# A hybrid decoder layer: z's projection in products of 512 columns, its Silu functions split around q's first copies, and two step quotas altered

## The chip, the core and the metric

The kernel runs on one core of a Trainium2 chip. A core has a matrix engine (TensorE, PE in the profile; its weight loads are shown apart as PEld), a vector engine (VectorE, DVE), an engine for functions and copies (ScalarE, ACT), a general one (GpSimd, POOL) and one that issues transfers (SyncE, SP). Each engine issues its instructions in a fixed order of its own, and engines wait for each other through semaphores. Products go to PSUM, a small memory that TensorE writes and DVE and ACT read; everything else lies in SBUF. The metric is the device time of one execution in microseconds; the kernel before is judged by the median of 3 runs.

## What is computed

One layer over 256 positions of 1024 channels, all in float32: a half-weighted SwiGLU network, then a Mamba-2 branch (SSD) and a differential attention branch side by side, gated and merged, then a second SwiGLU network, each with a norm before and behind it. The part that the change touches:

```python
u = rmsnorm(h, mix_pre_g[l])
z, xbc, dt_raw, q, k, v, gate_logits = jnp.split(u @ w_in[l], IN_SPLITS, axis=-1)
...
y = ssd_chunked(xh, dt, a_head, bm, cm)
y = (y + d_skip[:, None] * xh).astype(z.dtype)
y = y.reshape(b, L, SSD_D_INNER) * jax.nn.silu(z)
y = rmsnorm(y.reshape(b, L, SSD_GROUPS, SSD_D_INNER // SSD_GROUPS), 1.0).reshape(b, L, SSD_D_INNER) * norm_g
return y @ w_branch
```

z has 2048 columns, q and k 1024 each, the gates 2048. The SSD works in 4 groups of 8 heads, the attention in 8 heads.

## The kernel before

Every float32 weight and activation is split into a high part (rounded to the fast type float32r) and a low part (the rest), and a product is the sum hi x hi + hi x lo + lo x hi. Weights come from HBM in chunks of 1 MB through three `raw` buffers; for each half of a chunk ACT writes `whi` (a cast, line 250) and DVE writes `wlo` (a subtraction, line 253). `take()` hands out a chunk and prepares those that follow, three ahead. A raw buffer is loaded anew, on SP's queue, once its chunk is split.

There are two ways to make a 256-column chunk of the transposed projections. `mm_t` (line 294) writes both halves m of a chunk into one PSUM bank and takes 24 products of 256 columns for each half: 8 of `wh` with the high part of u, 8 with the low part, then 8 of `wl` with the high part. `mm_w` (line 306) lays the high and low parts of u side by side: for each half m, in a bank of its own, 8 products of `wh` with 512 columns and 8 of `wl` with 256 columns. Its bank then holds two sums, so ACT copies the right one to SBUF and DVE adds the left one. Three banks (`pj`) serve all of these. B, C, x and z are made by `mm_t`; q, k and the networks' gate and up by `mm_w`.

The mixer goes through its chunks in this order: v, B and C, x (8 chunks, tile `xs`), z (8 chunks, `pz` to `sz`), q and k in turn (4 chunks each, `pq` and `pk`), the gates (8 chunks, `pgt`), the SSD branch's output (8 chunks, `pws`), the attention branch's output (4 chunks, `pwd`), and the merge's output (`acc_mx`).

Behind these, in small steps, runs the background work. `Background.run(us)` (line 1298) adds `us` to an account and takes steps off a queue until the account is used up; each step names its own price. The queue holds first `cb_work`, then `ssd_work` for groups 0 to 3, then `ssd_norm`, then `att_work`. A group of `ssd_work` is: X (8 transposes `px` on TensorE, two DVE products), four E steps (each with eight 128-column functions and clips on ACT and DVE, an Exp of 512 columns on ACT and a product with `cbm` on DVE; every other one first loads `acb`, 512 KB, through POOL's queue), and `py` (32 products that read the E of all four steps, the last one first, then four DVE operations into `xs`). A group of `ssd_norm` multiplies `xs` by Silu of z, squares, sums into `ssum`, forms `pn` with two products by a matrix of ones, takes Ln and Exp, scales `xs` and splits it into `yh` and `yl`, which `pws` needs. `att_work` makes the heads' scores `psc`, the softmax, the transposes `pa`, the values `po` and the turned pairs `pto`.

What a chunk leaves to the background is set by four constants: `BG_US` 3.15 for each chunk of z, `QK_US` 2.4 for each of q and k, `GATE_US` 1.75 for each of 16 calls in the gates, `SSD_US` 1.55 for each of 16 calls in the SSD branch and 4 in the attention branch's first half.

ACT keeps one set of function tables at a time. `act_table(name)` loads another set and keeps the functions before and behind it apart; Silu is in one set, Exp and Ln in another, Sigmoid in a third. z's four Silu (one for each group, lines 1334 and 1335) stand between two such loads.

From x to k a scheduler chooses each engine's order by its own estimates of when things are ready. From the gates on, TensorE's order is the program's (`own_order(PE)`, line 1351); the other engines' orders are still the scheduler's.

Of the kernel before, what the change touches and what calls it, by code (L numbers as in the profile page):

```python
# [18 lines left out]
AF = mybir.ActivationFunctionType  # L19
# [4 lines left out]
EXP_LN = "natural_log_exp_and_others"  # L24
# [3 lines left out]
T = 256  # L28
# [12 lines left out]
WARM = 3  # L41
FILL = 2
TAIL = 3
BG_US = 3.15
QK_US = 2.4
GATE_US = 1.75
SSD_US = 1.55
DOWN = {"f1": "p q1 p p q2 p ppp", "f2": "q1 p q2 p q3 ppp"}
FIRST, LAST = (1, 2, 3, 5, 7, 6, 4), (1, 6, 7, 2, 5, 3, 4)
BREAK, STOP = object(), object()  # L50
# [3 lines left out]
def tile_hybrid_layer(ctx: ExitStack, tc: tile.TileContext, x, ffn1_pre_g, ffn1_w_gate, ffn1_w_up,  # L54
# [4 lines left out]
    nc = tc.nc  # L59
# [5 lines left out]
    def k4(shape, name, dt=F32):  # L65
        return sb.tile(shape, dt, tag="k4", name=name, bufs=K4_BUFS)
# [4 lines left out]
    def k2(shape, name, dt=F32):  # L71
        return sb.tile(shape, dt, tag="k2", name=name, bufs=K2_BUFS)
# [7 lines left out]
    def pj(name):  # L80

        return ps.tile([P, 512], F32, tag="pj", name=name, bufs=3)

    def pjt(name):

        return pj(name).rearrange("p (m t) -> p m t", m=2)

    def bg(shape, name):
        return ps.tile(shape, F32, tag="bg", name=name, bufs=5)
# [169 lines left out]
    def split_to(n):  # L259

        while len(splits) < min(n, len(units)):
            of, p = units[len(splits)]
            if p is not None:
                splits.append(of.split(p))
                continue
            for _ in split_steps():
                pass

    def ahead_of(i, n):

        n *= 4
        while n > 0 and i < len(units):
            n -= 4 if units[i][1] is None else 1
            i += 1
        return i

    def take(ahead=AHEAD):

        i = taken[0]
        taken[0] += 1  # L280
        split_to(ahead_of(i, ahead))
        (of, p), w = units[i], splits[i]
        splits[i] = None
        if p is not None:
            return w
        his, los = w
        nj = chunks[of][1][1] // 2
        return (lambda j: his[j // nj][:, j % nj, :], lambda j: los[j // nj][:, j % nj, :])
# [5 lines left out]
    def mm_t(acc, w, act, k0=0, first=True, last=True, ks=range(KD)):  # L294

        (wh, wl), (ah, al, _) = w, act
        acc = acc if isinstance(acc, list) else [acc[:, m, :] for m in range(2)]
        for m in range(2):
            cs = slice(m * P, (m + 1) * P)
            for j in ks:  # L300
                nc.tensor.matmul(acc[m], wh(j)[:, cs], ah(k0 + j), start=first and j == ks[0], stop=False)  # L301
                nc.tensor.matmul(acc[m], wh(j)[:, cs], al(k0 + j), start=False, stop=False)  # L302
            for j in ks:
                nc.tensor.matmul(acc[m], wl(j)[:, cs], ah(k0 + j), start=False, stop=last and j == ks[-1])  # L304

    def mm_w(dst, name, w, act, scale=None):


        (wh, wl), (ah, _, ahl) = w, act
        for m in range(2):  # L310
            acc = pj(f"{name}{m}")
            cs = slice(m * P, (m + 1) * P)
            for j in range(KD):
                if j:
                    nc.tensor.matmul(acc[:, :T], wl(j)[:, cs], ah(j), start=False, stop=False)  # L315
                nc.tensor.matmul(acc, wh(j)[:, cs], ahl(j), start=j == 0, stop=j == KD - 1)  # L316
                if not j:
                    nc.tensor.matmul(acc[:, :T], wl(j)[:, cs], ah(j), start=False, stop=False)
            if scale is None:
                nc.scalar.copy(dst[:, m, :], acc[:, T:])  # L320
                nc.vector.tensor_tensor(dst[:, m, :], acc[:, :T], dst[:, m, :], ALU.add)  # L321
            else:
                nc.scalar.activation(dst[:, m, :], acc[:, T:], AF.Copy, scale=scale)
                nc.vector.scalar_tensor_tensor(dst[:, m, :], acc[:, :T], scale, dst[:, m, :], ALU.mult, ALU.add)

    def mm_nat(acc, w, act, k0, first, last, late):
# [25 lines left out]
    order = mybir.DependencyInfo(mybir.DependencyClass.NoSync, mybir.DependencyReason.DATA)  # L352

    def act_table(name):
        f = nc.scalar.preload_act_table_set(name)
        for prev in act_since:
            tc.add_manual_dep(f.ins, prev, order, reason="activation table")
        act_since.clear()
        act_fence[0] = f.ins.name

    def act(*args, **kw):
        a = nc.scalar.activation(*args, **kw)
        if act_fence[0] is not None:
            tc.add_manual_dep(a.ins, act_fence[0], order, reason="activation table")
        act_since.append(a.ins.name)
# [65 lines left out]
    def new_u(tag):  # L431
        for i in range(2):
            uT[i] = sb.tile([P, 4, 2, T], F32R, tag="u8", name=f"u{i}_{tag}", bufs=2)

    act_u = (lambda j: uT[j // 4][:, j % 4, 0, :], lambda j: uT[j // 4][:, j % 4, 1, :],
             lambda j: uT[j // 4][:, j % 4, :, :])
# [594 lines left out]
    for i in range(4):  # L1031
        acc = pjt(f"pbc{i}")
        mm_t(acc, take(), act_u)
        dst = (bT, cT)[i // 2]
# [16 lines left out]
    sz = [None] * 4  # L1051
# [52 lines left out]
    def ssd_norm(groups):  # L1104

        def one(g):
            nc.vector.tensor_tensor(xs[g], xs[g], sz[g], ALU.mult)
            sq = k4([P, 4, T], f"sqy{g}")
            nc.scalar.activation(sq, xs[g], AF.Square)
            yield 1.2  # L1110
            nc.vector.tensor_tensor(sq[:, 0:2, :], sq[:, 0:2, :], sq[:, 2:4, :], ALU.add)
            nc.vector.tensor_tensor(sq[:, 0, :], sq[:, 0, :], sq[:, 1, :], ALU.add)
            ssum = k2([P, 2, T], f"ssum{g}", F32R)
            split(ssum[:, 0, :], ssum[:, 1, :], sq[:, 0, :])
            yield 1.5
            yield BREAK
            pn = bg([P, T], f"pn{g}")
            for i in range(2):
                nc.tensor.matmul(pn, ones_r, ssum[:, i, :], start=i == 0, stop=i == 1)
            rs = sq[:, 1, :]  # L1120
            act(rs, pn, AF.Ln, scale=1.0 / 512, bias=eps_c)
            act(rs, rs, AF.Exp, scale=-0.5)
            yield 0.1
            for c in range(4):
                n = col["ng"] + g * 4 + c
                nc.vector.scalar_tensor_tensor(xs[g][:, c, :], xs[g][:, c, :], cols_a[:, n:n + 1], rs,
                                               ALU.mult, ALU.mult)
            yh[g] = k4([P, 4, T], f"yh{g}", F32R)
            yl[g] = k4([P, 4, T], f"yl{g}", F32R)
            split(yh[g], yl[g], xs[g])  # L1130
            xs[g] = sz[g] = None
            yield 2.8

        todo = [one(g) for g in groups]
        under_way = []
        while todo or under_way:
            if todo and len(under_way) < 2:
                under_way.append(todo.pop(0))
            for w in list(under_way):
                us = next(w, None)  # L1140
                if us is None:
                    under_way.remove(w)
                else:
                    yield us
# [170 lines left out]
    back = Background()  # L1315
    back.add(cb_work())
    for g in range(4):
        xs[g] = k4([P, 4, T], f"xs{g}")
        for i in range(2):
            acc = pjt(f"pxs{g}{i}")  # L1320
# [5 lines left out]
    for g in range(4):  # L1326
        sz[g] = k4([P, 4, T], f"sz{g}")
        for i in range(2):
            acc = pjt(f"pz{g}{i}")
            mm_t(acc, take(), act_u)  # L1330
            nc.scalar.copy(sz[g][:, i * 2:i * 2 + 2, :], acc)
            back.run(BG_US)
    act_table(SILU)
    for g in range(4):
        act(sz[g], sz[g], AF.Silu)
    act_table(EXP_LN)
    back.add(ssd_norm(range(4)))
    for c in range(4):
        if c % 2 == 0:
            qT[c // 2] = k4([P, 4, T], f"q{c}")  # L1340
            kT[c // 2] = k4([P, 4, T], f"k{c}")
        o = (c % 2) * 2
        mm_w(qT[c // 2][:, o:o + 2, :], f"pq{c}", take(), act_u, 0.125)
        back.run(QK_US)
        mm_w(kT[c // 2][:, o:o + 2, :], f"pk{c}", take(), act_u)
        back.run(QK_US)
# [42 lines left out]
    for q in range(2):  # L1389
# [3 lines left out]

        natural(f"pws{q}", 4, lambda j: yh[j // 4][:, j % 4, :], lambda j: yl[j // 4][:, j % 4, :], gated, SSD_US)
    yh = yl = None
# [18 lines left out]
    for q in range(2):  # L1414
# [4 lines left out]
        def merge(b, acc):  # L1419
# [5 lines left out]
        natural(f"pwd{q}", 2, lambda j: oh[j // 4][:, j % 4, :], lambda j: ol[j // 4][:, j % 4, :], merge,  # L1425
                SSD_US if q == 0 else 0.0, (attended, lambda: turn_merged(2))[q])

    pg = load_gain(mix_post_g, "pg_mx")
    acc = [[bg([P, 512], f"acc_mx{b}{q}") for q in range(2)] for b in range(2)]
# [47 lines left out]
```

## Time and profile before

| | us |
|---|---|
| median of 3 runs | 737.97 (737.88 to 738.38) |
| the profiled execution | 737.54 |
| its span, first to last instruction | 735.8 |
| first z product to first q product | 289.28 to 343.87 |
| q and k, to the first gates product | 343.87 to 395.86 |
| gates, to the first product of the SSD branch | 395.86 to 447.68 |
| SSD branch, to the first product of the attention branch | 447.68 to 501.08 |

The page divides the span among engines, into forty slices, and along the chain of work that ended last. A tile's name in a row (`pz`, `sz`, `E`) says which step an instruction belongs to, and `<-` in brackets says what ended the idle time before it. Since TensorE's instructions overlap, the pace of its products is read from start to start and not from the duration of one.

### The profile page before, as it was taken

The page shows a single profiled execution, that of the slowest core. Times are in us where ns is not written, and L with a number is a line of the kernel's source. Part 1 is how long each engine was busy: PE and PEld are TensorE (multiplying, and loading weights), DVE is VectorE, ACT ScalarE, POOL GpSimd, SP SyncE. Part 2 cuts the span into 40 slices and gives each one's busy share as a digit, 9 for nine tenths or more (in the row PEclk, how much of TensorE's full clock was granted, in tenths as well). Part 3 has the DMA queues.
Part 4 walks back from the last instruction along what each step waited for, and adds up shares of the span by engine and source line. Part 5 has one row for each costly group of instructions (what it writes and reads, how often), then busy time and mean ns, then how long its engine had stood idle before and what let it go on. Part 6 is the DMA issues. An engine that isn't in the chain of part 4 may idle for free.

```text
span 735.8 us, 10869 instructions
## 1 busy us (share of the span) xinstructions
PE 726.4 (99%) x4211; PEld 628.1 (85%) x4211; DVE 591.9 (80%) x904; ACT 462.1 (63%) x777; POOL 38.6 (5%) x72
## 2 busy tenths in 40 slices
PE   8999999999999999999999999999999999999996
PEld 6888888888889999999888788888888888888874
DVE  7978768998677878787996998785784878779994
ACT  7657556665566565958975577782663657566562
POOL 2700000000300000000000000000010000000000
PEclk9999999999999999999999999999999999999998
DMA  8884674469353647567464664475470765664541
GB/s 299 229 261 150 218 229 171 155 216 348 118 172 117 201 143 226 192 188 226 146 219 154 202 222 138 152 238 191 127 241 34 229 199 153 222 217 143 188 168 57
DMA packets 94212, 137.96 MB, mean 187 GB/s; under 512 B 2684, under 2 KB 68304, under 8 KB 94160
## 3 DMA queue, kind: packets, MB, share of 16 engines
q1 hardware_dynamic: 91488, 129.51, 54.2%
q0 software_dynamic: 2368, 7.22, 3.1%
q8 instruction: 33, 0.54, 0.3%
q10 hardware_dynamic: 304, 0.53, 0.2%
q14 instruction: 19, 0.16, 0.1%
HBM read 136.17 MB, written 1.08 MB: 187 GB/s over the span
## 4 chain that ended last, share of the span: by engine, by line
PE 97%; DVE 2%; issue 1%; DMA 0%; ACT 0%; DVEq 0%
PE pup_f L316 9%; PE pg_f L316 9%; PE pgt L335 6%; PE pws L335 6%; PE acc_f1p L625 5%; PE acc_f2p L625 4%; PE pg_f L315 4%; PE pup_f L315 4%; PE pn_f L335 3%; PE pn_mx L335 3%; PE acc_mx L573 3%; PE pn_f L345 3%; PE pwd L335 3%; PE acc_f1p L573 3%; PE pz L302 2%; PE pxs L304 2%
## 5 line engine op out<-in xcount | busy, mean ns | idle before, releaser
L253 DVE TENSOR_TENSOR wlo<-raw,whi 128x1024 fp32r<-128x1024 f32 (+1 forms) x226 | 266.6, 1208 | 22.7 <-ACT whi L250 21.7
L250 ACT CAST whi<-raw 128x1024 fp32r<-128x1024 f32 (+1 forms) x225 | 226.2, 1044 | 18.1 <-DMA raw<-in_w_in_dram 3.8
L316 PE MATMUL pup_f<-u_f,whi 128*128 128x512 f32 x288 | 101.3, 396 | 0.0
L316 PE MATMUL pg_f<-u_f,whi 128*128 128x512 f32 x288 | 101.2, 396 | 0.0
L315 PE MATMUL pg_f<-u_f,wlo 128*128 128x256 f32 x252 | 70.6, 280 | 0.0
L315 PE MATMUL pup_f<-u_f,wlo 128*128 128x256 f32 x252 | 70.3, 279 | 0.0
L316 PEld LDWEIGHTS pup_f<-u_f,whi 128*128 128x128 f32 x288 | 52.8, 188 | 9.8
L316 PEld LDWEIGHTS pg_f<-u_f,whi 128*128 128x128 f32 x288 | 52.8, 188 | 9.6
L315 PEld LDWEIGHTS pg_f<-u_f,wlo 128*128 128x128 f32 x252 | 47.5, 188 | 1.7
L315 PEld LDWEIGHTS pup_f<-u_f,wlo 128*128 128x128 f32 x252 | 47.5, 189 | 1.6
L321 DVE TENSOR_TENSOR su_f<-pup_f,su_f 128x256 f32<-128x256 f32 x36 | 15.1, 420 | 26.0 <-ACT su_f L320 25.8
L130 ACT CAST wqh<-wt 128x1024 fp32r<-128x1024 f32 x20 | 21.0, 1052 | 23.2 <-DVE wt L122 23.2
L320 ACT COPY su_f<-pup_f 128x256 f32<-128x256 f32 x36 | 13.4, 373 | 35.1 <-PE pup_f L316 34.9
L335 PE MATMUL pgt<-whi,u_mx 128*128 128x512 f32 x128 | 33.1, 393 | 0.0
L301 PE MATMUL pxs<-u_mx,whi 128*128 128x256 f32 x128 | 31.7, 285 | 0.0
L302 PE MATMUL pz<-u_mx,whi 128*128 128x256 f32 x128 | 31.6, 284 | 0.0
L301 PE MATMUL pz<-u_mx,whi 128*128 128x256 f32 x128 | 31.6, 284 | 0.0
L302 PE MATMUL pxs<-u_mx,whi 128*128 128x256 f32 x128 | 31.4, 283 | 0.0
L335 PEld LDWEIGHTS pgt<-whi,u_mx 128*128 128x128 f32 x128 | 23.6, 188 | 5.4 <-issue 0.7
L1009 DVE SCALAR_TENSOR_TENSOR xs<-pxs,cols_b,xs 128x255 f32<-128x255 f32 (+2 forms) x48 | 21.9, 475 | 6.3 <-ACT xs L1006 5.9
L291 ACT CAST gh_f<-sg_f 128x512 fp32r<-128x512 f32 x18 | 11.2, 622 | 21.5 <-DVE sg_f L771 21.5
L302 PEld LDWEIGHTS pz<-u_mx,whi 128*128 128x128 f32 x128 | 24.5, 192 | 0.2 <-issue 0.2
(397 smaller groups left out, 1698.5 us busy)
## 6 DMA issues: line engine op xcount, KB each, us to landing
raw<-in_w_in_dram SPq DMA_DIRECT2D x40, 1024.0 KB, 5.4
raw<-in_ffn_w_down_dram SPq DMA_DIRECT2D x22, 1024.0 KB, 4.9
raw<-in_ffn_w_gate_dram SPq DMA_DIRECT2D x20, 1024.0 KB, 5.6
raw<-in_ffn_w_up_dram SPq DMA_DIRECT2D x20, 1024.0 KB, 5.4
raw<-in_ssd_w_branch_dram SPq DMA_DIRECT2D x8, 1024.0 KB, 5.3
acb<-acd POOLq DMA_DIRECT2D x8, 512.0 KB, 5.5
raw<-in_da_w_branch_dram SPq DMA_DIRECT2D x4, 1024.0 KB, 5.1
raw<-in_w_out_dram SPq DMA_DIRECT2D x4, 1024.0 KB, 5.0
```

The costliest lines, as they stand in the source:

```text
L130: nc.scalar.copy(hi, src)
L250: copy(hi[:, js, :], r[:, q * nj + j:q * nj + j + n, :])
L253: nc.vector.tensor_sub(lo[:, js, :], r[:, q * nj + j:q * nj + j + n, :], hi[:, js, :].bitcast(F32))
L301: nc.tensor.matmul(acc[m], wh(j)[:, cs], ah(k0 + j), start=first and j == ks[0], stop=False)
L302: nc.tensor.matmul(acc[m], wh(j)[:, cs], al(k0 + j), start=False, stop=False)
L315: nc.tensor.matmul(acc[:, :T], wl(j)[:, cs], ah(j), start=False, stop=False)
L316: nc.tensor.matmul(acc, wh(j)[:, cs], ahl(j), start=j == 0, stop=j == KD - 1)
L335: nc.tensor.matmul(acc, a(k0 + j), b(j), start=first and i == 0, stop=last and i == 11)
L345: nc.tensor.matmul(accs[b], x_(k0 + j), w_(j), start=first and j == 0 and w_ is wh and x_ is acts[b][0], stop=last and j == 3 and w_ is wl)
L573: nc.tensor.matmul(acc[b][q], x_[:, ts], w_(kt)[:, halves[q]], start=begin and i == 0 and kt == 0 and x_ is ah and w_ is wh, stop=i == n - ...
L625: nc.tensor.matmul(bank[p], x_, w_, start=p not in begun, stop=last and p in (1, 5, 6, 7))
L1009: nc.vector.scalar_tensor_tensor(dst[:, m, s:], acc[:, m, :T - s], cw(3 - s, c), dst[:, m, s:], ALU.mult, ALU.add)
```

## The change

z's chunks are made by `mm_w`, so each half has a bank of its own, an ACT copy and a DVE addition. Silu of z's first group stays behind z; the other three are put behind q's first chunk and, on ACT, behind the last copy of that chunk (`last_copy`), and the load of the Exp set and the start of `ssd_norm` follow them. `BG_US` goes from 3.15 to 2.5 and `SSD_US` from 1.55 to 1.95.

```diff
-BG_US = 3.15
+BG_US = 2.5
 QK_US = 2.4
 GATE_US = 1.75
-SSD_US = 1.55
+SSD_US = 1.95
...
+    last_copy = [None]
+
     def mm_w(dst, name, w, act, scale=None):
...
-                nc.scalar.activation(dst[:, m, :], acc[:, T:], AF.Copy, scale=scale)
+                last_copy[0] = nc.scalar.activation(dst[:, m, :], acc[:, T:], AF.Copy, scale=scale).ins
                 nc.vector.scalar_tensor_tensor(dst[:, m, :], acc[:, :T], scale, dst[:, m, :], ALU.mult, ALU.add)
...
-    def act(*args, **kw):
+    def act(*args, behind=None, **kw):
         a = nc.scalar.activation(*args, **kw)
+        if behind is not None:
+            tc.add_manual_dep(a.ins, behind.name, order, reason="behind a copy")
...
         for i in range(2):
-            acc = pjt(f"pz{g}{i}")
-            mm_t(acc, take(), act_u)
-            nc.scalar.copy(sz[g][:, i * 2:i * 2 + 2, :], acc)
+            mm_w(sz[g][:, i * 2:i * 2 + 2, :], f"pz{g}{i}", take(), act_u)
             back.run(BG_US)
     act_table(SILU)
-    for g in range(4):
-        act(sz[g], sz[g], AF.Silu)
-    act_table(EXP_LN)
-    back.add(ssd_norm(range(4)))
+    act(sz[0], sz[0], AF.Silu)
     for c in range(4):
...
         mm_w(qT[c // 2][:, o:o + 2, :], f"pq{c}", take(), act_u, 0.125)
+        if c == 0:
+
+            for g in (1, 2, 3):
+                act(sz[g], sz[g], AF.Silu, behind=last_copy[0])
+            act_table(EXP_LN)
+            back.add(ssd_norm(range(4)))
         back.run(QK_US)
```

## The prediction

> **What bounds the kernel now.** I read the page first, then the chain that ended last, then the busy time by stage.
>
> ```profile
> span 735.8 us, 10869 instructions
> PE 726.4 (99%) x4211; PEld 628.1 (85%) x4211; DVE 591.9 (80%) x904; ACT 462.1 (63%) x777; POOL 38.6 (5%) x72
> ...
> PEclk9999999999999999999999999999999999999998
> ...
> PE 97%; DVE 2%; issue 1%; DMA 0%; ACT 0%; DVEq 0%
> ```
>
> TensorE is busy for 99% of the span, holds 97% of the chain and has its full clock. So a product saved shortens the run, and a stall of TensorE lengthens it one for one; what the other engines do counts only where TensorE must wait. The pace of the two forms of product, and of the work set among them, is in the chain (start, us, what):
>
> ```profile
> 291.36 0.96 PE pz L304 x8
> 294.24 0.96 PE pz L304 x8
> 295.20 0.87 PE px L1061 x8
> ...
> 347.89 2.75 PE py L1093 x32
> ...
> 361.61 0.47 PE pq L316 x2
> 367.20 0.47 PE pk L316 x2
> ...
> 396.02 10.93 PE pgt L335 x48
> ```
>
> Half a z chunk takes 294.24 - 291.36 = 2.88 us for 24 products of 256 columns (0.12 each); a whole q or k chunk in the 512-column form takes 367.20 - 361.61 = 5.59. The three stages concerned (z; q and k; gates), as windows:
>
> ```profile
> 289.28:343.87 54.59, 54.57 (x474) 52.73 (x473) 42.86 (x73) 40.32 (x82) 2.65 (x6) 1.00 0.65 203
> 343.87:395.86 51.99, 51.99 (x334) 44.34 (x333) 44.95 (x70) 39.13 (x71) 1.57 (x3) 1.00 0.67 213
> 395.86:447.68 51.82, 51.82 (x264) 41.98 (x262) 49.02 (x85) 35.83 (x68) 0.53 (x1) 1.00 0.52 166
> ```
>
> The columns are length, PE, PEld, DVE, ACT, POOL, clock, DMA share, GB/s. TensorE is full in all three, and DVE is at 95% in the gates. Z plus the q/k stage can be added up: 8 x 5.76 + 8 x 5.59 + four py of 2.75 + four px of 0.87 = 105.3 of the 106.6 us. Almost nothing is waited for there, so the change has little to win beyond its products.
>
> **Z's products.** Each of 16 half chunks becomes 8 products of 512 columns and 8 of 256. Price: 8 x (5.76 - 5.59) = 1.3 us saved. From below it is 0 (if the new form ran in z at the old pace), from above 1.3; I take 1.3, since the rows are of the same operands and shapes. By the Trainium skill ("TensorE: Matmul & The Clock Gate", section "Back-to-back issue gap") an isolated product costs N/2.4 ns + 2.5 ns, which depends on columns almost alone; three of 256 against 512 + 256 would then save 2.5 ns x 128 = 0.3 us. The rows say 0.12 us a product for 256, where that formula has 0.109; I go by the rows, and by the page the sum below would be 1.0 us worse.
>
> **Z's evictions.** One copy of 512 columns becomes two copies and two additions of 256.
>
> ```profile
> L1331 ACT COPY sz<-pz x8: 559/586/590, 295.2 to 344.1; 128x512 f32<-128x512 f32 x8
> ...
> L320 ACT COPY k<-pk x8: 356/372/374, 356.3 to 395.8; 128x256 f32<-128x256 f32 x8
> L321 DVE TENSOR_TENSOR k<-pk,k x8: 408/418/424, 359.6 to 396.2; 128x256 f32<-128x256 f32 x8
> ```
>
> ACT gains 16 x 0.37 - 8 x 0.59 = 1.2 us of work, DVE 16 x 0.42 = 6.7. In z that is hidden: two Exp steps leave z (below), and DVE has 54.59 - 42.86 = 11.7 us free. If the cover were gone, TensorE would wait for one of the three accumulator banks; laid end to end, every bank is free 0.5 us or more before it is wanted, and the first py has its last E about 0.15 us ahead. I cost this part at 0 to 1.0 and take 0.
>
> **The steps that move.** At 2.5 us a chunk instead of 3.15, z gets 20 us of background steps instead of 25.2. In the order as built, z now ends with group 2's X and first acb load, two of its four E steps come directly behind z's last copy, and the other two (eight 128x128 functions, two Exp of 512, four clips and two products with cbm on DVE, and the second acb load) stand behind the whole block of Silu. Group 2's 32 py products, before within q's first chunk, stand behind q0, k0 and the first half of q1. Here is that block as it runs now:
>
> ```profile
> 343.87 0.40 PE L316 MATMUL pq<-u_mx,whi 128*128 128x512 f32 x1
> 344.07 0.59 ACT L1331 COPY sz<-pz 128x512 f32<-128x512 f32 x1
> 344.55 1.28 ACT L362 ACTIVATE E<-acb,acs 128x128 f32<-128x128 f32 x4
> 345.74 0.62 ACT L362 ACTIVATE E<-E 128x512 f32<-128x512 f32 x1
> 346.38 1.28 ACT L355 ACT_TABLE_LOAD   x1
> 346.39 0.96 DVE L1083 TENSOR_TENSOR E<-E,cbm 128x768 f32<-128x768 f32 x1 [0.85 <-ACT E L362]
> 347.67 3.90 ACT L362 ACTIVATE sz<-sz 128x1024 f32<-128x1024 f32 x4
> 348.76 1.23 DVE L1107 TENSOR_TENSOR xs<-xs,sz 128x1024 f32<-128x1024 f32 x1 [1.41 <-ACT sz L362]
> 351.58 1.28 ACT L355 ACT_TABLE_LOAD   x1
> 352.87 1.05 ACT L250 CAST whi<-raw 128x1024 fp32r<-128x1024 f32 x1
> 353.83 0.65 ACT L323 ACTIVATE q<-pq 128x256 f32<-128x256 f32 x2
> ```
>
> Time from q's first product, durations start to start. ACT's last z copy starts at 0.2 (344.07 - 343.87) and takes 0.28. Two E steps: 2 x 1.19 + 0.53 + 0.64 = 3.55, to 4.0. Table 1.29, to 5.3. Silu of z's first function 0.98, to 6.3. Then q0's two copies, 0.65 less the usual overlap of 0.1; their last product ended at about 5.8, so they don't wait: to 6.8. Three Silu, 2.93, to 9.75. Table, to 11.05. Two E steps, 2 x 1.19 + 0.53 + 0.62, to 14.6. DVE's product with cbm, 0.03 later, 0.96 long: 15.6. TensorE reaches py after 2.5 chunks of 5.59 = 14.0. So **py waits 1.6 us**, a wait that isn't there now. py's first product needs the last of the four E, so no part of it can start. From below this is 0, from above 2.7 (if DVE's xs products, 1.2 us in one piece, get in front of E's).
>
> By the Trainium skill ("ScalarE: Activation LUTs", "What ACT_TABLE_LOAD costs") a switch of sets is 1.28 us and a drain of 1.38. This trace shows the 1.28 and no drain: Silu starts 1.29 us after the load does. With drains the wait would be 1.6 + 2.8 = 4.4; that is a rival below.
>
> What the Silu hold up otherwise: q0's copies are no longer behind all four, so q0's bank is free at about 7.9 (behind DVE's product of xs with z, 1.2, and its own addition), and wanted by k0's second half at 8.4: 0.5 us to spare. The casts for k1's weights now come at 14.6, end at about 17.6 with DVE's half, and are wanted at about 22 (py 2.75, half of q1, px).
>
> The loads:
>
> ```profile
> acb<-acd POOLq DMA_DIRECT2D x8, 512.0 KB, 5.5
> ...
> raw<-in_w_in_dram SPq DMA_DIRECT2D x40, 1024.0 KB, 5.4
> ```
>
> Group 2's second acb is issued when z's last hi weights are free, 1.4 us before q begins, and has landed by 5, wanted at 11. A raw load is issued when the chunk three before it is split; the tightest is q3's, landed about 1 us ahead of its cast. Both cost nothing; without cover 1 to 2 us each.
>
> **The gates.** The norm of the SSD groups is one step further behind. All four pn pairs (two 256-column products each) now stand in the gates, one behind the gates' first 12 products, the next 12 later, two more on either side of the fourth chunk's second half.
>
> ```profile
> 390.27 0.47 ACT L362 ACTIVATE sqy<-pn,eps_c 128x256 f32<-128x256 f32 x1
> 390.77 0.42 ACT L362 ACTIVATE sqy<-sqy 128x256 f32<-128x256 f32 x1
> ...
> 392.93 1.05 ACT L291 CAST yh<-xs 128x1024 fp32r<-128x1024 f32 x1 [1.74 <-DVE xs L1126]
> ...
> 391.23 1.67 DVE L1126 SCALAR_TENSOR_TENSOR xs<-xs,cols_a,sqy 128x256 f32<-128x256 f32 x4 [0.39 <-ACT sqy L362]
> 394.01 1.23 DVE L292 TENSOR_TENSOR yl<-xs,yh 128x1024 fp32r<-128x1024 f32 x1 [1.12 <-ACT yh L291]
> ...
> 400.99 2.35 DVE L253 TENSOR_TENSOR wlo<-raw,whi 128x1024 fp32r<-128x1024 f32 x2
> ...
> 407.99 1.28 DVE L1383 TENSOR_TENSOR gt<-pgt,gb 128x512 f32<-128x512 f32 x2
> ```
>
> First wait: the third chunk's second half needs the bank that DVE's first gt frees, and gt stands behind both norms and the fourth chunk's lo weights. From pn's start: 0.4, Ln and Exp 0.96, DVE's four 1.70, yh 1.08, yl 1.14 = 5.3; the second group's four 1.70, yh 1.08, yl 1.14 = 9.2; two wlo 2.27 = 11.5; gt 0.68 and 0.15 to TensorE = 12.3. TensorE is there after 4 x 2.73 (10.93/4) plus two pn pairs of 0.24 = 11.4: 0.9 us of wait. The chain is long and each end in it rounded, so the bounds are 0 and 1.5, and I take their middle, **0.7**.
>
> ```profile
> L335 PE MATMUL pgt<-whi,u_mx 128*128 128x512 f32 x128 | 33.1, 393 | 0.0
> ...
> 406.52 0.42 DVE L292 TENSOR_TENSOR ssum<-sqy,ssum 128x256 fp32r<-128x256 f32 x1
> ...
> 406.99 0.19 PEld L1119 LDWEIGHTS pn<-ssum,ones_r 128*128 128x128 f32 x1 [0.24 <-DVE ssum L292]
> ```
>
> Second wait: the last pn needs ssum's lo half, and DVE has it behind the gt that evicts the 12 products directly ahead of that pn. No work of TensorE lies between. From the last product's start: 0.43 to DVE (the product's 0.39, and 0.04 to the next engine, an estimate by the 0.05 that follows), gt 0.60, ssum 0.42, 0.05 to the weights (406.94 to 406.99), 0.11 to the product = 1.6; TensorE would have been there at 0.35. **1.2 us**, 0.9 to 1.6. In return the wait of 0.2 that this row shows goes, since that pn now has its ssum early.
>
> **The SSD branch** at 1.95 a call instead of 1.55 gets heads' steps earlier relative to its products, DVE has 20% free there, and the tightest place I find (the last turned pair, before pwd) keeps 0.6 us. I take 0; without that cover, up to 1.
>
> **The sum.** -1.3 - 0.2 (pn) + 1.6 + 0.7 + 1.2 = +2.0. The profiled execution, 735.8 of span and 737.54 in all, becomes 739.5; the runs' median stands 0.4 above it, 737.97, so **739.9**.
>
> **The rivals.**
> - The start of q is covered: if each of the 29 instructions of ACT's block overlaps the next by 0.055 us more than the rows, E is there when TensorE is, and the 1.6 goes. That alone decides; above 14.0 us TensorE waits. Against it: the rows already are start to start. 739.9 - 1.6 = 738.3, and with the gates' first wait, a chain of the same kind, shortened to nothing too, 737.6: not slower. Chance 0.25.
> - No new wait anywhere, the products' gain alone: 737.97 - 1.5 = 736.5. The second gates wait, with no work between, speaks against it. 0.06.
> - DVE falls behind in z: 6.7 us of additions come in pieces that each wait for an ACT copy, while the next casts queue behind it. From 0.15 us of delay on, the first py waits, then each bank. Price 0.2 to 2: about 741.5. 0.12.
> - The new products save next to nothing, as columns alone would have it: 739.9 + 1.0 = 740.9. 0.05. A table switch drains ACT (+2.8): 742.7. 0.02.
> - The forecast: 0.50, between 739.0 and 740.9.
>
> **How the numbers follow.** About 0.2% (1.5 us) is what a measurement can tell from no change: slower is above 739.45, faster below 736.5. Faster: 0.06. Same: the first rival's 0.25 and a fifth of the forecast's 0.5, 0.35. Slower: the rest, 0.59. The range 737.0 to 741.4 leaves out the second rival below and the worst of the third and the drains above.
>
> **What would show it.** In the profile after: sixteen z half chunks 2.80 us apart; in the first q1 chunk an idle TensorE before py that ends on DVE's E; DVE's E preceded on ACT by the load of the Exp set at about 9.75 us into q; in the gates, a wait for gt before the third chunk's second half and one for ssum at the last pn. It is wrong if py starts without a gap, if the wait lies in z, or if the last pn does.

## The result and the profile after

The changed kernel takes 741.23 us, median of 6 runs (740.76 to 741.95); the kernel before took 737.92 on the same chip, median of 6. The ratio is 1.0042, with a 95% interval of 1.0032 to 1.0052: 3.3 us slower. The forecast was 739.9, and the time lies inside its range, 0.2 under the upper end of 741.4. The profiled execution took 741.83.

The page after, first lines and chain:

```profile
span 740.1 us, 10623 instructions
PE 728.0 (98%) x4083; PEld 622.8 (84%) x4083; DVE 596.4 (81%) x920; ACT 461.6 (62%) x785; POOL 38.6 (5%) x72
...
PE 92%; DVE 3%; ACT 3%; issue 1%; DMA 0%; DVEq 0%; SPq 0%; ACTq 0%
```

128 products fewer, and 4.3 us more of span. TensorE's share of the chain falls from 97% to 92%, and ACT comes into it with 3%: TensorE now waits on chains that run through ACT and DVE. The view of TensorE's waits from 285 to 545 us says where (total, times, longest). For the kernel before it is empty.

```profile
PE py L1097 <- DVE E L1087: 1.4, 1, 1.4
PE pn L1123 <- DVE ssum L292: 1.0, 1, 1.0
PE pgt L337 <- DVE gt L1388: 0.6, 1, 0.6
```

The stages, as windows after (z; q and k; gates; SSD branch), and of before the one stage not yet shown, the SSD branch; the columns are length, PE, PEld, DVE, ACT, POOL, clock, DMA share, GB/s:

```profile
290.13:343.45 53.32, 53.32 (x346) 45.64 (x345) 45.72 (x79) 36.90 (x76) 2.65 (x5) 1.00 0.65 199
343.45:396.46 53.01, 51.62 (x330) 43.87 (x328) 45.65 (x76) 43.03 (x82) 1.59 (x3) 1.00 0.65 212
396.46:447.10 50.64, 49.01 (x234) 39.24 (x233) 43.47 (x74) 29.39 (x53) 0.53 (x1) 1.00 0.50 161
447.10:505.12 58.02, 57.90 (x313) 48.46 (x312) 48.87 (x89) 46.69 (x96) 0.00 (x0) 1.00 0.57 187
sum 214.99, PE 211.85 PEld 177.20 DVE 183.71 ACT 156.02 POOL 4.77; mean PE 52.96 PEld 44.30 DVE 45.93 ACT 39.00 POOL 1.19
```

```profile
447.68:501.08 53.40, 53.40 (x279) 44.73 (x279) 42.45 (x73) 41.05 (x79) 0.00 (x0) 1.00 0.59 201
```

From z's first product to the attention branch's first, before took 54.59 + 51.99 + 51.82 + 53.40 = 211.8 us and after takes 215.0: 3.2 more, which is the 3.3 of the medians. The other 1.1 between the two spans lies outside: 0.85 of it ahead of z's first product (290.13 against 289.28), where nothing was changed. So below, executions are compared over these four stages, called "the four stages". Single stages can't be compared alone: the quotas move whole steps, with their products, from gates to SSD branch (264 products become 234, 279 become 313).

The forecast named three waits. The first, in q1, as the timeline shows it (start, duration, engine, line, what):

```profile
348.73 1.06 ACT L364 ACTIVATE sz<-sz 128x1024 f32<-128x1024 f32 x1
349.69 0.64 ACT L325 ACTIVATE q<-pq 128x256 f32<-128x256 f32 x2
350.22 2.95 ACT L364 ACTIVATE sz<-sz 128x1024 f32<-128x1024 f32 x3
...
353.17 1.28 ACT L357 ACT_TABLE_LOAD   x1
...
354.47 1.28 ACT L364 ACTIVATE E<-acb,acs 128x128 f32<-128x128 f32 x4
355.66 0.62 ACT L364 ACTIVATE E<-E 128x512 f32<-128x512 f32 x1
356.18 1.26 ACT L364 ACTIVATE E<-acb,acs 128x128 f32<-128x128 f32 x4
...
357.35 0.61 ACT L364 ACTIVATE E<-E 128x512 f32<-128x512 f32 x1
...
358.00 0.96 DVE L1087 TENSOR_TENSOR E<-E,cbm 128x768 f32<-128x768 f32 x1 [0.73 <-ACT E L364]
```

```profile
357.22 0.40 PE L318 MATMUL pq<-u_mx,whi 128*128 128x512 f32 x1
359.01 0.44 PE L1097 MATMUL py<-E,X 128*64 128x256 f32 x2 [1.39 <-DVE E L1087]
```

One reads down ACT's column: Silu, q0's two copies, three Silu, the table, two E steps, with nothing idle between. The table is loaded 353.17 - 343.45 = 9.72 us into q, DVE's E ends at 358.96, 15.5 into q, and py starts with it. The product ahead of py takes 0.23 (512 columns; 0.35 for it and one of 256, by 5.59 / 16), so TensorE lost 359.01 - 357.22 - 0.23 = 1.56. (The waits view says 1.4, since it ends a product where its data have passed through; the loss is read start to start.) E starts 1.30 after the table's load of 1.28: no drain.

The two waits in the gates:

```profile
409.76 1.07 PE L337 MATMUL pgt<-whi,u_mx 128*128 128x512 f32 x4
...
410.72 1.28 DVE L1388 TENSOR_TENSOR gt<-pgt,gb 128x512 f32<-128x512 f32 x2
...
411.46 1.20 PE L337 MATMUL pgt<-whi,u_mx 128*128 128x512 f32 x4 [0.64 <-DVE gt L1388]
...
420.07 0.28 PE L1123 MATMUL pn<-ssum,ones_r 128*128 128x256 f32 x1
420.27 0.69 DVE L1388 TENSOR_TENSOR gt<-pgt,gb 128x512 f32<-128x512 f32 x1 [0.80 <-PE pgt L337]
420.88 0.41 DVE L292 TENSOR_TENSOR ssum<-sqy,ssum 128x256 fp32r<-128x256 f32 x1
...
421.35 0.39 PE L1123 MATMUL pn<-ssum,ones_r 128*128 128x256 f32 x1 [0.99 <-DVE ssum L292]
```

The second half of the third chunk starts behind DVE's first gt: the four products at 409.76 take 4 x 0.228, so the next was due at 410.67, and came 0.79 later. The last pn product starts 1.28 behind its partner, where 0.12 is usual, with gt and then ssum on DVE between: 1.16 lost. In return the pn pair that waited before is free: its two products and the step to the next took 0.42 there, 0.24 elsewhere, so 0.2 is gained.

What the forecast did not have is in the SSD branch. After:

```profile
474.77 0.60 PE L1244 MATMUL pto<-ident,o 128*128 128x128 f32 x4
...
475.31 0.50 PE L1170 MATMUL psc<-k,q 64*128 64x128 f32 x4
...
475.47 0.68 ACT L1256 ACTIVATE oh<-pto,g 128x512 fp32r<-128x512 f32 x1
...
476.06 0.38 PE L1170 MATMUL psc<-k,q 64*128 64x128 f32 x2
...
476.21 0.74 DVE L1257 SCALAR_TENSOR_TENSOR ol<-pto,g,oh 128x512 fp32r<-128x512 f32 x1
...
477.00 0.29 PEld L1170 LDWEIGHTS psc<-k,q 64*128 64x128 f32 x2 [0.53 <-DVE ol L1257]
477.00 0.49 PE L1170 MATMUL psc<-k,q 64*128 64x128 f32 x2
...
477.85 1.19 PE L337 MATMUL pws<-whi,yh 128*128 128x512 f32 x4
```

and the same steps before:

```profile
466.18 0.60 PE L1240 MATMUL pto<-ident,o 128*128 128x128 f32 x4
...
466.54 1.16 PE L335 MATMUL pws<-whi,yh 128*128 128x512 f32 x4
...
469.44 0.50 PE L1166 MATMUL psc<-k,q 64*128 64x128 f32 x4
...
471.06 1.21 PE L335 MATMUL pws<-whi,yh 128*128 128x512 f32 x4
```

psc (a head's scores) and pto (a turned pair) take their tiles from one set of banks, `bg`. Before, 12 products of pws stood between the turned pair and the next scores, and ACT's `oh` and DVE's `ol` read the pair's bank meanwhile. After, the scores stand directly behind the pair, and the weights of the last four products wait 0.53 us for `ol`. The 16 score products (two heads) take 477.85 - 475.31 = 2.54 us in place of 471.06 - 469.44 = 1.62, and the pair itself 0.54 in place of 0.36: 1.1 us in all. The wait is the smaller part of it: start to start, TensorE stands still for 0.28 (the last product of the first half head starts at 476.50 and takes 0.22, the next starts at 477.00). The greater part: each head's scores come in two half heads, and their products start two and two, 0.01 apart in the trace, while both banks are there; the first head's eight take 0.75 us (475.31 to 476.06). When the bank of one half is held, the other half's products go alone, and the second head's eight take 1.79, where they took 0.86 before (470.20 to 471.06).

What stands ahead of the pair counts too. By the kernel `bg` has five banks, and the values po, a turned pair and the scores of two heads are six tiles. In the change these three stand right behind one another, so the last half head must wait until DVE has read the pair's bank (`ol`) or that of po, whichever comes first.

### The profile page after: what moved, and what is told of

The parts are those of the page before. It is cut to its first block, busy times and chain, and to the rows that moved or that the text cites. A ratio compares the mean times of both kernels' runs of the same rounds, so it can differ in the third digit from the quotient of the medians.

```text
span 740.1 us, 10623 instructions
## 1 busy us (share of the span) xinstructions
PE 728.0 (98%) x4083; PEld 622.8 (84%) x4083; DVE 596.4 (81%) x920; ACT 461.6 (62%) x785; POOL 38.6 (5%) x72
## 4 chain that ended last, share of the span: by engine, by line
PE 92%; DVE 3%; ACT 3%; issue 1%; DMA 0%; DVEq 0%; SPq 0%; ACTq 0%
PE pup_f L318 9%; PE pg_f L318 9%; PE pws L337 6%; PE acc_f1p L629 5%; PE pgt L337 5%; PE pz L318 4%; PE pg_f L317 4%; PE pup_f L317 4%; PE acc_f2p L629 3%; PE pn_f L347 3%; PE pn_f L337 3%; PE pn_mx L337 3%; PE acc_mx L577 3%; PE acc_f1p L577 3%; PE pwd L337 3%; PE pxs L304 2%
## 5 line engine op out<-in xcount | busy, mean ns | idle before, releaser
L318 PE MATMUL pz<-u_mx,whi 128*128 128x512 f32 x128 | 44.8, 400 | 0.0
L317 PE MATMUL pz<-u_mx,wlo 128*128 128x256 f32 x112 | 31.3, 280 | 0.0
```

## The experiments

The theory at this point: z's products save what the rows said, 1.2 to 1.3; the split of Silu costs nothing; all that is lost comes from the two quotas, which move whole steps and so make discrete waits.

### The old quotas under the new code

```diff
-BG_US = 2.5
+BG_US = 3.15
-SSD_US = 1.95
+SSD_US = 1.55
```

> The changed kernel with the quotas of before (BG_US 3.15, SSD_US 1.55): z's new products and the split Silu alone. Theory (the quotas make all the new waits): no wait before py in q1, none of 0.8 before the third gates chunk's second half, none of 1.2 at the last pn, none behind pto0 in the SSD branch; z's products save 1.2; laid end to end by the profiles' durations there is left a wait of about 0.5 in z's sixth chunk (a bank that DVE frees late) and one of about 0.8 in q1's second half behind DVE's addition to k0: 737.4, about 0.5 under before, at most 738.0. Rival 1 (the split evictions of z or the split Silu cost the time, the quotas nothing): about 741, as the change. Rival 2 (z's products save nothing of themselves): 738.7.

738.32 us against 737.96 of before, ratio 1.0004 (0.9995 to 1.0014): no difference from before, and 3 us better than the change. All three waits are gone, and these two stand in the waits view:

```profile
PE pq L318 <- DVE k L323: 0.7, 1, 0.7
PE pz L318 <- DVE sz L323: 0.4, 1, 0.4
```

Both are where they were expected. The time was given too low, by a slip of addition: start to start they are 0.82 and 0.53, and -1.2 + 0.8 + 0.5 is +0.1, not -0.5. With the old quota, then, z's gain is real and is given back: 0.5 of it by z's own evictions (DVE frees a bank of z late), and 0.8 in q1, behind DVE's addition to k0. The run with z alone, further below, shows that this second wait belongs to the split Silu.

### The quotas alone in the kernel before

```diff
-BG_US = 3.15
+BG_US = 2.5
-SSD_US = 1.55
+SSD_US = 1.95
```

> The kernel before with the change's quotas alone (BG_US 2.5, SSD_US 1.95); z in products of 256 columns and the four Silu in one block. Theory (the quotas make the waits, and neither z's evictions nor the split have a part in them): the waits in the gates (0.8), at the last pn (1.1) and behind pto0 (1.2 with the scores that run singly) are all here; with the Silu in one block the wait before py becomes one of 3.0 in k0's second half, as in the run with the changed quotas and one block; z saves nothing: 5 to 6 slower than before, 743.2 to 744.2. Rival (the evictions' work on DVE makes the norms late): the waits in the gates are below 0.4, at most 741.

745.70 against 738.07, ratio 1.0105 (1.0088 to 1.0122). The waits in the gates are the same without z's new evictions and without the split, so neither makes them:

```profile
PE pk L316 <- DVE q L324: 3.0, 1, 3.0
PE pn L1119 <- DVE ssum L292: 1.0, 1, 1.0
PE pgt L335 <- DVE gt L1383: 0.6, 1, 0.6
```

The loss is 7.6, 1.5 over the upper expectation. About half of that surplus lies behind the long wait and is told of at the end.

### z in halves of 256 columns again, all else as changed

```diff
-            mm_w(sz[g][:, i * 2:i * 2 + 2, :], f"pz{g}{i}", take(), act_u)
+            acc = pjt(f"pz{g}{i}")
+            mm_t(acc, take(), act_u)
+            nc.scalar.copy(sz[g][:, i * 2:i * 2 + 2, :], acc)
```

> The changed kernel with z's chunks made by mm_t again (24 products of 256 columns a half, one copy of 512 columns), all else as changed. Theory (z's products save 1.2 and their evictions cost nothing, the waits are the quotas'): 1.2 to 1.5 slower than the change, 742.5, and z's pace back at 2.88 us a half chunk; the waits before py, in the gates and behind pto0 all stay, each within 0.3. Rival 1 (the evictions' 6.7 us of DVE work push E or the norms late and so make the waits): the waits shrink, and the time falls to 739.5 or less.

742.71, 1.5 slower than the change. z's stage takes as long as before, 54.58:

```profile
289.62:344.20 54.58, 54.58 (x474) 52.74 (x473) 40.91 (x65) 36.39 (x68) 2.69 (x5) 1.00 0.64 196
```

The wait before py is 1.6 in the waits view in place of 1.4, and those in the gates are unchanged at 1.0 and 0.6. DVE has 4.8 us less to do in z (40.91 against 45.72), and no wait shrinks.

### One quota at a time

BG_US back to 3.15, SSD_US left at 1.95:

```diff
-BG_US = 2.5
+BG_US = 3.15
```

> The changed kernel with BG_US 3.15, SSD_US left at 1.95. Theory: the waits before py (1.6), in the gates (0.8) and at the last pn (1.2) go, since group 2's E and the norms stand one step earlier again; but the attention's steps then also stand earlier in the SSD branch, and the last head's scores psc come directly behind another head's first turned pair, waiting for DVE's three operations on it: a wait of 3 to 4 us there in place of 0.4. Sum: 741 to 742, no faster than the change, with all of it in the SSD branch (first pws to first pwd 57 us against 53.4 of before). Rival 1 (BG_US alone is the loss, SSD_US costs nothing): 737.5. Rival 2 (the split Silu or z's evictions are the loss): 741, with the loss in z, q and k.

742.65, ratio 1.0054 (1.0035 to 1.0074). The three waits are gone, the two of the run with the old quotas are back (0.7 and 0.4 in the view), and the wait in the SSD branch has grown: 2.0 by the view, start to start 2.2 in place of 0.28. That is below the 3 to 4 expected, while the time is over the expectation by 0.65; what came on top stands at the end:

```profile
PE psc L1170 <- DVE ol L1257: 2.0, 1, 2.0
```

SSD_US back to 1.55, BG_US left at 2.5:

```diff
-SSD_US = 1.95
+SSD_US = 1.55
```

> The changed kernel with SSD_US 1.55, BG_US left at 2.5. Theory: the waits before py, in the gates and at the last pn stay (3.5 together), the one of psc behind pto0 goes (0.4, and 0.7 of scores that run singly), but at 1.55 a call the steps that BG_US has put off don't fit, and the first pwd products wait for the turned pairs: 1.5 for the first two heads and 0.6 further on. Sum 741 to 742.5; the SSD branch alone (first pws to first pwd) is back at 53.5 to 54.5, and the attention branch's output is longer by 2. Rival (SSD_US 1.95 costs the SSD branch 1.2 and nothing takes its place): 740.0.

742.40, ratio 1.0050 (1.0035 to 1.0065). The scores run two and two again, 16 in 1.61, though here too they stand right behind a turned pair (479.97 behind 479.44): 12 products of pws stand between po and that pair, and DVE's last reading of po's bank ends at 479.58, ahead of the half heads that would have had to wait. By these rows it is the three in a row that cost, and not the pair alone. The three waits stay, and pwd waits for turned pairs that are now late:

```profile
502.66 0.74 PE L337 MATMUL pwd<-whi,oh 128*128 128x512 f32 x2 [0.87 <-ACT oh L1256]
...
510.67 1.08 PE L337 MATMUL pwd<-whi,o 128*128 128x512 f32 x3 [0.47 <-ACT o L1256]
```

Neither quota is the loss by itself. 2.5 leaves more steps to the later stages, which 1.55 can't finish in time and 1.95 places badly. Each undone alone leaves the kernel 1.2 to 1.4 us slower than the change; undone together, they give 3 us back.

### Quotas between the two

With the order that each quota gives and the durations of the profiles, 2.8 and 1.7 should leave no step late and no scores right behind a pair whose bank is still being read.

```diff
-BG_US = 2.5
+BG_US = 2.8
-SSD_US = 1.95
+SSD_US = 1.7
```

> The changed kernel with quotas between the two (BG_US 2.8, SSD_US 1.7). Theory: at 2.8, z still gets fewer steps than before, so its bank isn't waited for (0.5 in the run with the old quotas), but group 2's E stands before the Silu block and the norms one step earlier, so py, gt and ssum aren't waited for; at 1.7 no scores stand right behind a turned pair whose bank DVE has not freed, and the pairs before pwd are in time. Left: a wait of about 0.2 in k's stage. The change's z gain of 1.2 and the 0.2 of the old pn wait and some 0.3 elsewhere are then kept: 736.2, 1.7 under before, and at most 736.9. Rival (the split evictions and Silu cost about as much as the products save, as the run with the old quotas may be read): 738.

737.11, median of 11, against 738.16 of before: ratio 0.9985 (0.9976 to 0.9994), 1.1 faster than before (0.4 to 1.8) and some 4 faster than the change. It beats both kernels, though by less than expected. The view of TensorE's waits is empty again, and the four stages add up to:

```profile
sum 210.44, PE 210.43 PEld 176.37 DVE 183.05 ACT 154.33 POOL 4.74; mean PE 52.61 PEld 44.09 DVE 45.76 ACT 38.58 POOL 1.19
```

That is 1.4 below before's 211.8.

The same with SSD_US 1.95, so that one number differs:

```diff
-SSD_US = 1.7
+SSD_US = 1.95
```

> As the run with the quotas between, but SSD_US 1.95 as changed: one number differs. Theory: everything to the gates' end is alike to 0.2 us; in the SSD branch the last head's scores stand right behind another head's turned pair and wait for its bank, for 1.5 to 3 us, and their products run singly instead of in pairs (0.5 to 0.9 more): 738.8 to 739.5, 2.5 to 3.3 slower than with 1.7. Rival (SSD_US costs nothing of itself, the order of scores and turned pairs doesn't matter): 736.2.

740.77, ratio 1.0036 (1.0023 to 1.0050), 3.7 slower than with 1.7. One line in the waits view:

```profile
PE psc L1170 <- DVE ol L1257: 2.2, 1, 2.2
```

This separates the two quotas cleanly: SSD_US alone puts the scores right behind values and turned pair and pays for it. How long the wait is depends on what DVE has in hand at that moment: start to start it is 0.28 in the change and 2.3 here, where DVE has three `wlo` (3.5 us) and an eviction of pws in hand ahead of `ol`. The time is over the expectation; see the end.

And the same quotas between, with z made by mm_t again (the edit as above):

> Quotas between (BG_US 2.8, SSD_US 1.7) and the split Silu, z by mm_t in products of 256. Theory: no wait but one of 0.2, as with the new products; what is left of the gain of the run with the quotas between is not z's: 737.11 + 1.2 = 738.3, within 0.4 of before. Rival (the gain over before comes from the quotas or the split): 737.1.

738.25, ratio to before 1.0001 (0.9991 to 1.0010); no wait of TensorE. Against the run with the new products 738.25 - 737.11 = 1.1: so the gain over before is z's products, and the quotas between and the split Silu, taken together, cost nothing and bring nothing. This run doesn't part the two; those below do.

### The split of Silu

All four Silu at z's end, quotas as changed:

```diff
-    act(sz[0], sz[0], AF.Silu)
+    for g in range(4):
+        act(sz[g], sz[g], AF.Silu)
+    act_table(EXP_LN)
+    back.add(ssd_norm(range(4)))
...
-        if c == 0:
-
-            for g in (1, 2, 3):
-                act(sz[g], sz[g], AF.Silu, behind=last_copy[0])
-            act_table(EXP_LN)
-            back.add(ssd_norm(range(4)))
```

> The changed kernel with all four Silu, the load of the Exp set and the start of the norms at z's end again, quotas as changed. Theory: py's wait of 1.6 goes, since the block no longer stands between q0's copies and group 2's last E steps in such a way, but q0's copies are behind the block and both E steps ahead of it, and k0's second half waits 2.7 for q0's bank; the waits in the gates, at the last pn and behind pto0 stay: 742.5, 1.2 slower than the change. So the split takes some of the price of the low quota away. Rival (the split Silu are themselves the loss before py): 739.6.

744.07, ratio 1.0078 (1.0064 to 1.0092), 2.8 slower than the change, where 1.2 was expected. In the waits view py is gone and this stands in its place:

```profile
PE pk L318 <- DVE q L326: 2.8, 1, 2.8
```

So the split doesn't make py's wait out of nothing: it exchanges a wait of 2.8 for one of 1.4. Quotas between, z in the new products, and Silu in one block, shown against the kernel before:

```diff
-BG_US = 3.15
+BG_US = 2.8
-SSD_US = 1.55
+SSD_US = 1.7
...
-            acc = pjt(f"pz{g}{i}")
-            mm_t(acc, take(), act_u)
-            nc.scalar.copy(sz[g][:, i * 2:i * 2 + 2, :], acc)
+            mm_w(sz[g][:, i * 2:i * 2 + 2, :], f"pz{g}{i}", take(), act_u)
```

> Quotas between and z's new products, the four Silu in one block as before. Theory: q0's copies stand behind the block and behind the E steps that the lower quota leaves to it, so k0's second half waits 2.7 for q0's bank, and nothing else waits: 737.11 + 2.5 = 739.6 (739.2 to 740.2). So the split is what lets the quota be lowered. Rival (the split is worth nothing, or costs): 737.1 or less.

739.02, ratio 1.0012 (1.0003 to 1.0022), 1.9 slower than with the split. The wait is where it was expected but 1.7 long, not 2.7, and the time 0.2 below the range that was given:

```profile
PE pk L316 <- DVE q L324: 1.7, 1, 1.7
```

### z alone in the kernel before

Only the last part of the diff just shown, quotas 3.15 and 1.55, one block of Silu.

> The kernel before with z's products in 512 columns alone; Silu in one block and quotas as before. Theory: z's products save 1.2, a bank in z's sixth chunk is wanted 0.5 before DVE frees it, and q0's copies stand behind the block of four Silu, so that k0's second half waits 0.7 (and q1's no longer 0.8): 737.5, 0.4 under before. Rival 1 (the evictions cost as much as the change lost): 740 or more. Rival 2 (without the split, q0's copies are late by the whole block, 2.7): 739.7.

737.50, ratio 0.9993 (0.9984 to 1.0002), as expected in sum but not in its parts: the wait for q0's bank isn't there. What is left in the waits view is z's own, for DVE's additions (0.53 start to start, and -1.27 + 0.53 is -0.7):

```profile
PE pz L316 <- DVE sz L321: 0.4, 1, 0.4
```

The run with the old quotas under the new code differs from this one in the split alone. It took 738.32, which is 0.8 more (1.0 when each is set against its own runs of before), and the wait of 0.82 in q1 that it has isn't here. So the split isn't free: at 3.15 it costs 0.8 to 1.0. At 2.8 it saves 1.9, and at 2.5 it saves 2.8 (1.4 of that in waits, start to start; the rest is taken up at the end).

## Why the prediction was right, and where it was not

Half of the chance was put on 739.0 to 740.9, which the time misses by 0.3. That it still lies in the range is partly luck: the range reached to 741.4 for rivals such as DVE falling behind in z, which didn't come; what filled it was a term that had been put at nothing.

- **z's products, -1.3.** z's stage went from 54.59 to 53.32, 1.27. Undoing them costs 1.5 in the change and 1.1 at the quotas between. The rival that they save next to nothing is out, and with it the 0.3 that was worked out from the formula of the Trainium skill for an isolated product ("TensorE: Matmul & The Clock Gate", "Back-to-back issue gap").
- **Their evictions, 0.** Right for the change, which has no wait in z; so the rival that DVE falls behind in z is out too. The bound of 1 was needed: with the old quota the cover is gone, and TensorE waits 0.5 (start to start) for a bank of z.
- **py, 1.6.** Measured 1.56, with each step of ACT's column within 0.1 us of the sum, and TensorE there at the 14.0 that was forecast. The rival that overlaps would cover it is refuted by that column. The wait goes with BG_US (gone with 3.15 and with 2.8), not with z's form.
- **The gates, 0.7 and 1.2.** By the rows, the third chunk's second half starts 0.8 late, and ssum costs 1.16. Both waits go when BG_US does. The durations had given 0.9 for the first, and 0.7 was the middle of its bounds, so that this one came so near is in part chance.
- **The drains of a table switch** (a rival): E follows the load by 0.02 us. None.
- **The SSD branch, 0 and at most 1: mis-sized, and at 1.1 just beyond its own bound.** It cost 1.1, the greater part of what was missing between +2.0 and +3.3. The step that failed was "gets heads' steps earlier relative to its products, DVE has 20% free there", with the last turned pair before pwd as the tightest place. A share of free time over a stage says nothing of which two steps stand next to each other. At that pair nothing is waited for in the change; the tight place was values, a turned pair and another two heads' scores in a row, six tiles for five banks. That SSD_US makes this order was shown by the two runs that differ in it alone. That the row of three decides, and not the pair alone, rests on the rows of these runs and of the one with SSD_US 1.55; no run moved only po.
- **A stall counts one for one.** So it did in the changed kernel, whose waits are at most 1.6. In three of the runs with waits of 2.0 and more it didn't, as the last section shows.

The sum of what the rows show is -1.27 + 1.56 + 0.8 + 1.16 + 1.1 - 0.2 (pn) = 3.15, against 3.2 in the four stages and 3.3 in the medians. So the terms that were forecast came out within 0.1 each, and one that was costed at nothing was worth 1.1.

Not settled: why laying durations end to end gave a wait of 0.7 for q0's bank in the run with z alone that isn't there, and 2.7 where 1.7 was seen. No run tested it.

## What to carry to other kernels

A quota of background work moves whole steps, so its cost jumps: look for the steps of the bound engine that share a set of buffers or wait on one chain, count the buffers, and see what will stand between the steps, not what share of another engine is free. A gain of 1.3 us in one stage survived only with the quotas set anew around it; two quotas that were changed together had to be judged together, since each undone alone only moved the loss. And where a function block is split to free an engine earlier, ask what stands behind the second part: here it was group 2's last E steps.

## What was not expected of the hardware

**A wait can cost twice.** Behind some long waits TensorE's granted clock halves: in three of the profiled runs, once each, and in no other before its last 5 us. In the run with quotas between and SSD_US 1.95, the window that begins 0.9 us behind the end of psc's wait, and in the quotas alone, that which begins 1.2 behind the wait in k0 (columns as above; the clock is the third from the right):

```profile
473.40:476.80 3.40, 3.40 (x9) 2.72 (x9) 2.66 (x6) 2.28 (x7) 0.00 (x0) 0.51 0.65 239
```

```profile
356.90:360.30 3.40, 3.40 (x12) 2.89 (x11) 3.40 (x8) 3.40 (x9) 0.53 (x1) 0.51 0.35 86
```

In the run with BG_US alone undone the clock is half for 3.41 us from 469.76 on, 1.5 behind the end of psc's wait:

```profile
469.00:473.00 4.00, 4.00 (x12) 3.08 (x12) 3.90 (x7) 2.60 (x5) 0.00 (x0) 0.60 0.62 237
```

For 3.4 us the clock is half, which costs half of that, 1.7, beside the wait itself (2.2, 3.0 and 2.0 by the view): in the last of these runs, the 12 products of pws from 469.06 on take 4.43 us, and 4.43 - 12 x 0.228 = 1.7. But in the profiled run with Silu in one block, the wait of 2.8 at the same place as the 3.0 left the clock whole:

```profile
354.20:360.00 5.80, 5.80 (x33) 5.08 (x34) 5.35 (x10) 5.80 (x14) 0.53 (x1) 1.00 0.36 119
```

So the length of the wait alone doesn't decide it. Executions of one kernel differ in this: with SSD_US 1.95 at the quotas between, two of four took 739.8 and 740.0 at a mean clock of 0.998, and two 741.5 and 741.8 at 0.995 and 0.996; the run with Silu in one block took 742.9 in the profiled execution, at 0.998, and 744.1 to 744.4 in the others, at 0.994 to 0.997. (The mean of 0.997 is seen in executions of the kernel before too, so it tells little by itself.) That accounts for much of the surplus of these runs over what was expected of them, and not for all: the fastest execution of the quotas alone, at 0.998, took 744.98, still 0.8 over the upper expectation. The Trainium skill ("TensorE: Matmul & The Clock Gate", "Part 1: The HAM clock gate") has the array's activity judged in windows of about 3.4 us that run on by themselves, and half the clock behind an idle one. The length of the halved stretch and the differing executions agree with that. The section speaks of a whole idle window; here a halved stretch followed a wait of 2.0. That the wait brings it about is argued from its place in three runs; no run tested it apart. The waits of up to 1.6 in the changed kernel left the clock at 1.00 in all four stages.

**Small products lose their pairing.** Score products took 1.62 us for 16 when both half heads' banks were there, and 2.54 when one of the banks was held, of which 0.28 was TensorE standing still: a held bank slows the products that don't need it too, when these would have run beside those that do.
